# Grouped attention on three engines: a new written-out order, three planner constants, and the heads whose exponential terms are added

## The chip, the cores and the metric

The kernel runs on one core of a Trainium2 chip. A core has TensorE (PE in the profile) for matmuls, ScalarE (ACT) for exponentials, VectorE (DVE) and GpSimd (POOL) for elementwise work, and SyncE (SP), whose queue issues most transfers. The metric is device time in microseconds (us) of one launch. The kernel before took a median of 354.96 us in 3 runs (354.9 to 355.17).

## The reference

Attention with 8 batches, 8 query heads, 2 key/value heads, 1024 positions and a head size of 64, all in float32:

```python
for g in range(n_kv_heads):
    q_group = q[:, g*4 : g*4+4]               # four query heads share one key head
    scores = scale * np.matmul(q_group, k_group.transpose(0, 1, 3, 2))
    attn = np.exp(scores - np.max(scores, axis=-1, keepdims=True))
    attn = attn / (np.sum(attn, axis=-1, keepdims=True) + 1e-08)
    output[:, g*4 : g*4+4] = np.matmul(attn, v_group)
```

So there are 64 heads (batch x query head), each with 1024 x 1024 exponentials. The kernel leaves out the maximum, which the quotient doesn't need for these sizes.

## The kernel before

**Tiling.** A head is cut into 8 score tiles. A score tile has 128 partitions and 2 x 512 columns: line 754 makes it with two matmuls, one for the even query rows against one block of 128 keys and one for the odd rows against the block four further on. The tile lies in one of three slots of PSUM (`sp0` to `sp2`). The exponential of a tile is made in one of two ways.

- On ScalarE: one activation (line 764) writes the tile `pt` in bfloat16.
- On VectorE: one pass (line 775) turns the scores into 16-bit integers `yt`, whose bits read as bfloat16 are a rough exponential. Three steps refine it: line 782 (`zh`) masks the mantissa into `zt`, line 789 (`two`) masks the exponent into `et`, and line 798 (`mul`) multiplies `yt` by `zt`. The exponential is then the sum of two terms, `et` + `zt`. Two tiles usually share a chain (class `Chain`), so that each step works on 2048 columns.

**Values.** Line 816 multiplies 128 queries of a tile with 128 values, which have 64 columns and a column of ones, so that the 65th column sums the exponentials. Eight such pieces of 128 queries make a head. A `pt` tile costs eight matmuls. A VectorE tile costs sixteen, because both terms are multiplied, except in the last TAIL heads: there a fourth step (line 803, `add`) adds the two terms first, and the tile costs eight (lines 267 and 710). Seven pieces share a PSUM bank. VectorE then takes the reciprocal of their sums (line 881, `rec`) and multiplies (line 890, `norm`), and SyncE's queue stores the head (line 894). The first head and the last go through lines 836 and 856, eight matmuls for each tile and term.

**GpSimd.** It multiplies a part of the columns that line 798 would have to (line 732, `gmul`). The part is cut from the end of a chain's columns, and VectorE's own multiply gets what is left. The method `gpsimd` (line 207) is called where VectorE begins a pass or a reciprocal, since VectorE then reads PSUM for a while. It is told how long that lasts, and sizes the part by `w = int((until - at - M_GFIX) / M_GCOL) // GSTEP * GSTEP`, where `until` is the window's end plus M_GOVER and `at` its start plus M_GLEAD. The part waits for the VectorE instruction before the window. GpSimd's queue also issues the loads that cast queries, keys and values to bfloat16 (line 517); SyncE's queue transposes them (lines 576 and 586).

**What sets the order.** The text ORDER (line 64) holds one letter for each decision. For TensorE, `A` is a score tile for ScalarE, `a` to `d` one for VectorE (of the head at hand or of later ones), `V` up to three or four value matmuls, `E` and `L` the values of the first and last head, `F` a matmul that only keeps TensorE busy, `W` waiting. For VectorE, `p` and `P` are a pass, `r` and `R` a reciprocal, `n` a normalization, a digit the next step of that chain, `x` closes a chain early, `i` waits. With `P` and `R` a normalization follows beside the same part of GpSimd. The class `Plan` reads the letters with its constants (lines 11 to 46, in nanoseconds) and turns them into a list of events with planned times. These times fix the sequence on each engine and the place of each transfer in its queue: a query transpose stands 11 us ahead of its head's first score (line 685). On the chip the engines follow their sequences and wait for each other by semaphores, whatever the planned times. M_REC is the planned cost of a reciprocal; M_GFREE is how far a part may reach into VectorE's next instruction before the plan charges for it (line 313).

Of the kernel before, what the change touches and what calls it, by code (L numbers as in the profile page):

```python
# [29 lines left out]
M_D1 = 1.042  # L30
M_D2 = 0.521
M_D4 = 0.261
M_REC = 90
M_GLEAD = 160
M_GFIX = 190
M_GCOL = 1.88
M_GOVER = 100
M_GLATE = 900
M_GFREE = 125
M_ISSUE = 850  # L40
M_OVER = 5000
NEED = 5150
M_GFREE = 125
M_OVER = 5000
NEED = 5150
M_NORM = 531
# [3 lines left out]
PB = 7  # L50
NPIECE = 8
GRAIN = 3
TAIL = 4
CHN = 2
LONG = 6
GFROM = 2
# [5 lines left out]


ORDER = """
AaApFFFFFWFFAWWWWWWWWWWWWWWWWWWWWaWWWWWWWWWWApEEWWAW0WWWbWWWWApEEWWAWW0WWWaEpAEWWA0WWAFWWWWbFF0FE0AE
pAWWWWWWWAR0AWWWWWWWWWaWWWnWWWWWWpWWWWAVVVVVVARnb0VVVVpAVVVVVA0aWWWWApVVVVVVVVAR0AVb0VVVPVVAVVVVnVVA
b0VVVpAVVVVVA0AWWW0WbVVVRVpVVVVAVVVnVVA0bWWWApVVVVVVVVA0AWW0WbVVVRVPVVVVAVVVnVVA0bWWWApVVVVVVVVA0cWW
0WAVVVRVPVVVVAVVVnVAb0WWWWWApVVVVVVVVA0AWW0WWcVVVRpVVVVVAVVnVVVA0bWWWApVVVVVVVVA1cWWWArVPVVVVVVVAnWc
WWA0VpVVVVVVVA0WWcWWApVVVVVVVVAR0AWWWc0VVVVVPVAVVVVVcnAVpVVVAVVV1WVVAcR0WWWWAVPVVVVVVVAnWWAWc0V1VVVV
VpVVAVVVA0bVRVPVVAVVVVVnAA0WVVVV1VVVVVV0AV0VVVVAbVRVPVAVVVVVVVnVAb0WWAVpVVVVVVVVVA0WWWbWA0VVVVVRVPVV  # L70
VAVVVVbnAVpVVVAVVVVV0VVAc1VVVApVVVVVVVA1WbWWWApVVVVVVVVVVA0r1bWWAPVVVVVVVVVAncW0WWAVVVV0VVARVPVVVVVV
AWWnWWWWbA1VVVVVpVVAVVVA1bVRVPVVVAVVVVnVAA00VVVVVAW0WbVVVpVVVVVVAVVrV0cAVpVVVVVAVV0VVAb0VVVVAPVVVVVV
VAncWWW0WAVVVVpVVVVAVVV0VAb0VVVRVpAVVVVVAnbWWW0WAVVVpVVVVAVVVRV1Ab1VVVVAPVVVVVVAnWbWWA0ipVVVVVVVVAR1
cVV1VAVPVVVVAVVVnVVA0bWWWApVVVVVVVVAR1cWWWAPVVVVVVVVVAnbWW0WAVVpVVVVVVVAVV0VVAAR1VVVVVnVVVVVV1cAVpVV
VVVVVA0WWWbWAVpVVVVVVVARWW1WbWWAVPVVVVVVVAnWWcWWA0VVV0VVVVVApVVVVVARW1WbWWAVPVVVVVVVAnWWcWWA0VVVpVVV
VVAVVRV1bAVPVVAVVVVnVAA0VVVV0VVVV0cWAVpVVVVVVVVARW1WbWWAVPVVVVVVVVVAnWcWWA0VVVVpVVVVVVAVV0VcARVPVVVA
VVVnVVA1bVVVpVAVVVVVA01cWWWApVVVVVVVVA0cVARPVVVVVVAnWAV0VVVVV1cWApVVVVVVVVA0cWWWA1VVVVRVPVVVAVVVVnVA
c0WWWApVVVVVVVVAR1cWWWAPVVVVVVVVAnAV1VVVVVVVc2AVpVVVVVVVVVArW0Wc1WWAVVVPVVVVVVAVVnVVVA2cVVpAVVVVVAR0
bVVPVAVVVVVVnAV2AAV1VVVV0VVVVVVA1bVRVPVVVVVAVVnVVVA0cVVVpAVVVVVAR1bWWWAPVVVVVVVVAncWWWA1VVVpVVVAVVVV
0VA1cVRVPVVAVVVVVVnVAa1WWWAVpVVVVVVVVVA0WWWcA1VVVVVpVVVVAVVVVV0VVAbWWWARpVVVVVVVAnAV1VVVVVV0VVVVA0cV  # L80
VVRVPAVVVVVVAnaWW0WWAVVVpVVVVVVAVV0VVA0bVVVVRPVVAVVVVAnWAV0VVVVVVV0bWAVpVVVVVVVARW0WbWAVPVVVVVVVAnWW
bWA0VVVVVpVVVVAVVVV0VVARb0WWWAVPVVVVVVVVVAnWWAWb0VVVVVpVVVAVVVVV0VVARb0WWWWAVPVVVVVVVAnWWbWWA0VVVVpV
VVAVVVV0VVA0bWWWARVPVVVVVVVAnWWbWWA0VVVVpVVVVAVVV0VVA0bWWWARVpVVVVVVVAnWbWWA0VVVVpVVAVVVVV0VVARb0WWW
AVPVVVVVVVAnWWaWWA0VVVVVpVVVVAVVVV0Aa0VVVVVpAVVVVVVAR0WbVVAPVVVVVVVAnAV1VVVVVV0VVAR0aVVVPVVAVVVAnbVi
VipVVVAVVVV0Ab0VVVVVApVVVVVVA0WbWWApVVVVVVVVVVAR1bWWWAPVVVVVVVVVAncWW0WAVpVVVVVVVA0WAVVRV1VVVVVVnVAb
1VVVVpAVVVVVA0bWWWARPVVVVVVVVAnbWWW1WAVVV1VVVVApVVVVVVA0WWbWWARpVVVVVVVVAnaWW1WAVVVpVVVVVAVV0VA0bVVV
RAPVVVVVVAnaV1AVVpVVVVAVVV0VVVAR0bWWWAPVVVVVVVVAnAV1VVVVVVV1VaAipVVVVVVVVVVA0WbWWARPVVVVVVVVVVAnAV1V
VVVVV1bWApVVVVVVVVVARW0WbWWWAPVVVVVVVVAnWbVV1VAVpVVVVVVAV0VVVVA0bWWRWAPVVVVVVVVAnAV1VVVVV1VVbAipVVVV
VVAWWRWW0WcAPVVVVVVVVAnWAWWWb1VVVVpVVVVAVVV0VVAR0cWWWAPVVVVVVVVAnWAWWWb1VVVV1VVVVApVVVVVAW0WWWcWARpV
VVVVVVVAnWcWWWA1VVVVpVVVVAVVV0VVA0cWWWARPVVVVVVVVAnbWWWA1VVVV1VVVVApVVVVVARWW0WbWAPVVVVVVVVAncWWWA1V  # L90
VVpVVVVVAVV0VVVAR0bWWWAPVVVVVVVVAnAV1VVVVVc1WAVpVVVVVVVA0WWbWARPVVVVVVVVAnWAV1VVVVVVb0WAVVpVVVVVVVVA
WW0WWWWcAVRPVVVVVVVAVnVVVb1AVVVpVVAVVVVA1cV0VVpAVVVVVVA1aWWWWARPVVVVVVVVAnbWWW1WAVVVpVVVVAVVVrV2AAnV
VVVV0VV1VVVVA0bVVVVVApVVVVVVVARWnWbWAVpVVVVVVVVVA0WAWWWA0VVVVVV0VVVVVVVrVnVbA0VVVVVVVVVApVVVVVAVV0VV
VAaVVVpVVAVVVVVV0AbWWWArPVVVVVVVVA0AVVnVVVVV0VVVVAAV0VVVVVVVVVVVARnaVVVpVAVVVVVVVVRA0AVnVVVVVV0VVVVV
VA0AVVVVVVVRVV0VVVVVVVVAanWWAVpVxVVVVVVVVVVAR0AWnWAVVV0VVVV0VVVVVL0LLLRnLLLLFFRFn
"""


# [29 lines left out]
class Plan:  # L128
# [78 lines left out]
    def gpsimd(self, s, t, window):  # L207
# [11 lines left out]
        at = max(t, s.tG)  # L219
        until = t + window + M_GOVER  # L220
        at += M_GLEAD
# [19 lines left out]
    def dve(self, s):  # L241
# [14 lines left out]
        if what in "rR":  # L256
            _, _, lo, hi = s.norms[0]
            if s.dq and s.dq[0][0] <= t + M_REC:
                self.gpsimd(s, t, M_REC + 1134 + (M_NORM if what == "R" else 0))
                s.host = True  # L260
            s.ev.append((t, "rec", (lo, hi), None, None))
            end = t + M_REC
            s.dlast = lo
            s.norms[0] = (end, "norm", lo, hi)
        elif what in "pP":
            _, sl, j, c = s.dq.pop(0)
            n = len(STEPS) if j >= nj - TAIL else 3
            if s.open and s.open.nsteps != n:
# [33 lines left out]
        else:  # L302
# [7 lines left out]
            if cols:  # L310
                s.ev.append((t, kind, None, ch.id, n, cols))
                end = at + M_FIX + cols * rate
                end += max(0, s.tB - at - M_GFREE)
            if kind == "zh":
# [26 lines left out]
    def pe(self, s):  # L341
# [4 lines left out]
        if kind in "Aabcd":  # L346
# [12 lines left out]
            else:  # L359
                s.dcount[j] += 1  # L360
                if j == 0:
                    s.twice.append(c)
                if j < nj - TAIL:
                    s.mms[j] += 1
# [73 lines left out]
def kernel(  # L438
# [265 lines left out]
    def terms(j, par, only=range(NC)):  # L704

        for ci in only:
            c = ci if par == 0 else (ci + NH) % NC
            if (j, c) in where:
                ch, i = where[(j, c)]
                if j < NJ - TAIL:  # L710
                    yield ci, et[ch].bitcast(BF16)[:, i, par, :]
# [217 lines left out]
```

## Time and profile before

| | |
|---|---|
| median of 3 runs | 354.96 us |
| profiled execution, its own time | 354.69 us |
| its span, first to last instruction | 352.9 us |
| first exponential on ScalarE begins | 6.22 us |
| last exponential ends | 348.12 us |
| VectorE's last normalization ends | 349.83 us |
| median time of a store to its landing | 3.1 us |
| TensorE clock granted | 1.00 |

The page gives busy time for each engine, a chain of work followed back from the last instruction (each step goes to what released it), and groups of instructions by line and tile. A row such as `L775 DVE TENSOR_SCALAR yt<-sp 128x1024 ... x143 | 172.6, 1207 | 0.6` says: line 775, VectorE, `yt` from `sp`, shape, 143 instructions, 172.6 us busy in all, 1207 ns for one, and 0.6 us of idle time before them. Records of one engine overlap here, one instruction draining while the next begins, so what an instruction costs is the distance from its start to the next start, which is shorter than its record.

### The profile page before, as it was taken

The page shows a single profiled execution, that of the slowest core. Times are in us where ns is not written, and L with a number is a line of the kernel's source. Part 1 is how long each engine was busy: PE and PEld are TensorE (multiplying, and loading weights), DVE is VectorE, ACT ScalarE, POOL GpSimd, SP SyncE. Part 2 cuts the span into 40 slices and gives each one's busy share as a digit, 9 for nine tenths or more (in the row PEclk, how much of TensorE's full clock was granted, in tenths as well). Part 3 has the DMA queues.
Part 4 walks back from the last instruction along what each step waited for, and adds up shares of the span by engine and source line. Part 5 has one row for each costly group of instructions (what it writes and reads, how often), then busy time and mean ns, then how long its engine had stood idle before and what let it go on. Part 6 is the DMA issues. An engine that isn't in the chain of part 4 may idle for free.

```text
span 352.9 us, 14128 instructions
## 1 busy us (share of the span) xinstructions
PE 344.6 (98%) x6247; PEld 223.8 (63%) x6247; DVE 344.3 (98%) x519; ACT 344.3 (98%) x373; POOL 204.1 (58%) x188
## 2 busy tenths in 40 slices
PE   8899999999999999999999999999999999999995
PEld 4456666666666666666666666666666666666664
DVE  4999999999999999999999999999999999999995
ACT  5999999999999999999999999999999999999994
POOL 3157656676577666676766566666657676663000
PEclk9999999999999999999999999999999999999999
DMA  6799666478866987669639756679567885454133
GB/s 150 133 151 151 135 124 136 91 141 146 133 126 124 140 157 132 120 115 154 154 61 181 138 124 115 135 108 180 109 114 130 165 141 112 101 101 114 27 93 121
DMA packets 96430, 44.84 MB, mean 127 GB/s; under 512 B 61152, under 2 KB 95072, under 8 KB 95584
## 3 DMA queue, kind: packets, MB, share of 16 engines
q1 hardware_dynamic: 94128, 31.48, 43.1%
q0 software_dynamic: 2096, 12.19, 24.0%
q8 instruction: 49, 0.80, 1.1%
q10 hardware_dynamic: 144, 0.26, 0.2%
q14 instruction: 13, 0.11, 0.1%
HBM read 27.13 MB, written 28.97 MB: 159 GB/s over the span
## 4 chain that ended last, share of the span: by engine, by line
DVE 67%; PE 21%; ACT 8%; issue 3%; DVEq 0%
DVE yt L775 35%; PE ops L816 10%; DVE et L789 8%; PE sp L754 8%; ACT pt L764 8%; DVE zt L798 7%; DVE ost L890 7%; DVE zt L782 7%; DVE rec L881 2%; PE ops L619 1%; PE sp L856 1%; PE sp L642 0%; DVE kt L663 0%; PE ops L654 0%; PE ops L642 0%
## 5 line engine op out<-in xcount | busy, mean ns | idle before, releaser
L764 ACT ACTIVATE pt<-sp 128x1024 bf16<-128x1024 f32 x369 | 341.8, 1034 | 0.5 <-PE sp L754 0.4
L732 POOL TENSOR_TENSOR zt<-yt,zt 128x464 bf16<-128x464 bf16 (+5 forms) x131 | 173.4, 1324 | 107.7 <-DVE et L789 35.5
L816 PE MATMUL ops<-va,pt 128*128 128x65 bf16 x2848 | 175.1, 194 | 0.0
L754 PE MATMUL sp<-qt,kt 64*128 64x512 bf16 x1024 | 171.0, 382 | 3.2 <-ACT pt L764 1.5
L775 DVE TENSOR_SCALAR yt<-sp 128x1024 uint16<-128x1024 f32 x143 | 172.6, 1207 | 0.6 <-PE sp L754 0.5
L816 PEld LDWEIGHTS <-pt 128*128 128x128 bf16 x2848 | 127.7, 97 | 31.9 <-issue 31.9
L816 PE MATMUL ops<-va,zt 128*128 128x65 bf16 x1120 | 130.9, 194 | 0.0
L816 PE MATMUL ops<-va,et 128*128 128x65 bf16 x1072 | 121.7, 194 | 0.0
L816 PEld LDWEIGHTS <-zt 128*128 128x128 bf16 x1120 | 89.9, 97 | 12.3 <-issue 12.1
L816 PEld LDWEIGHTS <-et 128*128 128x128 bf16 x1072 | 84.2, 98 | 20.6 <-issue 20.6
L754 PEld LDWEIGHTS <-kt 64*128 64x128 bf16 x1024 | 49.2, 93 | 54.8 <-issue 32.5
L782 DVE TENSOR_SCALAR zt<-yt 128x2048 uint16<-128x2048 uint16 x72 | 50.1, 696 | 0.1
L789 DVE TENSOR_SCALAR et<-yt 128x2048 uint16<-128x2048 uint16 x72 | 49.6, 691 | 0.0
L798 DVE TENSOR_TENSOR zt<-yt,zt 128x832 bf16<-128x832 bf16 (+7 forms) x69 | 45.1, 654 | 0.0
L890 DVE TENSOR_TENSOR ost<-ops,rec 128x448 f32<-128x448 f32 (+2 forms) x73 | 44.3, 607 | 0.2
L517 POOL DMA_DIRECT2D qd<-in_q_dram x33 | 20.2, 613 | 4.2 <-PE sp L754 3.3
L881 DVE RECIPROCAL rec<-ops 128x7 f32<-128x7 f32 (+2 forms) x73 | 14.2, 195 | 0.0
L517 POOL DMA_DIRECT2D kd<-in_k_dram x8 | 5.4, 670 | 5.4 <-PE sp L754 5.4
L619 PE MATMUL ops<-warm 128*128 128x128 bf16 (+1 forms) x23 | 4.5, 339 | 1.2 <-DVE warm L511 1.2
L517 POOL DMA_DIRECT2D vd<-in_v_dram x8 | 5.0, 621 | 0.2 <-issue 0.2
L803 DVE TENSOR_TENSOR zt<-et,zt 128x2048 bf16<-128x2048 bf16 (+1 forms) x4 | 4.4, 1090 | 0.1
L619 PEld LDWEIGHTS <-warm 128*128 128x128 bf16 x23 | 2.0, 114 | 3.7 <-issue 2.5
(38 smaller groups left out, 25.2 us busy)
## 6 DMA issues: line engine op xcount, KB each, us to landing
out_dram<-ost SPq DMA_DIRECT2D x64, 256.0 KB, 3.1
qd<-in_q_dram POOLq DMA_DIRECT2D x29, 256.0 KB, 5.0
kt<-kt SPq DMA_DIRECT2D x30, 64.0 KB, 3.1
va<-vd SPq DMA_DIRECT2D x30, 64.0 KB, 3.7
kd<-in_k_dram POOLq DMA_DIRECT2D x7, 256.0 KB, 5.6
vd<-in_v_dram POOLq DMA_DIRECT2D x7, 256.0 KB, 5.2
qt<-qd SPq DMA_TRANSPOSE x63, 4.5
qd<-in_q_dram POOLq DMA_DIRECT2D x5, 128.0 KB, 3.7
```

Of the source, the lines that this page charges most:

```text
L517: return nc.gpsimd.dma_start(out=t.rearrange("(a x) d -> a (x d)", a=128), in_=src.rearrange("(a x) d -> a (x d)", a=128),)
L619: nc.tensor.matmul(ops[bank][:, lo : lo + cols], lhsT=warm[:, 0:128], rhs=warm[:, 0:cols], start=not beside, stop=True, skip_group_check=b ...
L732: gps = nc.gpsimd.tensor_tensor(out=z, in0=flat(yt[j])[:, lo : lo + w], in1=z, op=ALU.mult)
L754: now = nc.tensor.matmul(sps[x][:, half, :], lhsT=t[lo : lo + D, c // NH, ci % NH * 128 : (ci % NH + 1) * 128], rhs=qt[j][lo : lo + D, 0, ...
L764: exps.append(nc.scalar.activation(out=p, in_=where_s[(j, c)], func=AF.Exp, scale=scale))
L775: vec = nc.vector.tensor_scalar(out=yt[ch][:, i, :, :], in0=where_s[c], scalar1=EXP_A, scalar2=EXP_B, op0=ALU.mult, op1=ALU.add,)
L782: vec = nc.vector.tensor_scalar(out=zt[j][:, 0:c], in0=yt[j][:, 0:c], scalar1=0x7F, scalar2=0x3F00, op0=ALU.bitwise_and, op1=ALU.bitwise_or,)
L789: vec = ins = nc.vector.tensor_scalar(out=et[j][:, 0:c], in0=yt[j][:, 0:c], scalar1=0x7F80, scalar2=None, op0=ALU.bitwise_and,)
L798: vec = nc.vector.tensor_tensor(out=z, in0=flat(yt[j])[:, 0 : cols[0]], in1=z, op=ALU.mult)
L816: nc.tensor.matmul(ops[plan.group_of[x] % 2][:, lo : lo + D + 1], lhsT=p[:, qs * 128 : (qs + 1) * 128], rhs=va[(b * G + h // HPG) % NVA][: ...
L881: vec = nc.vector.reciprocal(out=to, in_=sums)
L890: vec = nc.vector.tensor_tensor(out=to, in0=o, in1=by, op=ALU.mult)
```

## The change

The text ORDER is replaced as a whole. Three constants of the plan change (M_REC 90 to 115, M_GOVER 100 to 60, M_GFREE 125 to 85), and TAIL goes from 4 to 3: the two terms are added in heads 61, 62 and 63 and no longer in head 60. No other code changes. Of the 31 lines of the text, the first three and the last are shown.

```diff
-M_REC = 90
+M_REC = 115
 M_GLEAD = 160
 M_GFIX = 190
 M_GCOL = 1.88
-M_GOVER = 100
+M_GOVER = 60
 M_GLATE = 900
-M_GFREE = 125
+M_GFREE = 85
 M_ISSUE = 850
 M_OVER = 5000
 NEED = 5150
-M_GFREE = 125
+M_GFREE = 85
...
-TAIL = 4
+TAIL = 3
 CHN = 2
...
-AaApFFFFFWFFAWWWWWWWWWWWWWWWWWWWWaWWWWWWWWWWApEEWWAW0WWWbWWWWApEEWWAWW0WWWaEpAEWWA0WWAFWWWWbFF0FE0AE
-pAWWWWWWWAR0AWWWWWWWWWaWWWnWWWWWWpWWWWAVVVVVVARnb0VVVVpAVVVVVA0aWWWWApVVVVVVVVAR0AVb0VVVPVVAVVVVnVVA
-b0VVVpAVVVVVA0AWWW0WbVVVRVpVVVVAVVVnVVA0bWWWApVVVVVVVVA0AWW0WbVVVRVPVVVVAVVVnVVA0bWWWApVVVVVVVVA0cWW
...
-VA0AVVVVVVVRVV0VVVVVVVVAanWWAVpVxVVVVVVVVVVAR0AWnWAVVV0VVVV0VVVVVL0LLLRnLLLLFFRFn
+AaApFFFFWWWWFAWWWWWWWWWWWWWWWWWWWWWWWWWWWWaWWWWWWWWWWApEEWWAW0WWWbWWWWApEEWWAW0WWWaWWWWApEEWWA0WWbFF
+WAFFpFEAWWW0WWWAAE0W0WWWWWWWWWWWWWWWaRAnWWWWRWWWPWAVVVVVVVVnA0bWWWWApVVVVVVVVA0aWVpAVVVVVAR0bVVA0VVV
+pVVVAVVVVnVAb0VVVApVVVAV0VVVVA0bVVRVPVVVVVAVVnbV0AVpVVVVVAVV0VVA0bVVRVPVAVVVVVVAnbW0WWAVVpVVVVVVAV0VV
...
+RVV0VVVVVVVVAnAVVV0VVVVVVVVVVVVVVRAnaWWWApVVVVVVVVVxVA0ArVnVVVVVVV0VA0AVVV0VVVVVLLRnLLLLLWWLFFRFn
```

Counted over both texts: `A` 369 before and 370 after, `a` to `d` 143 and 142, `p` and `P` 143 and 142, `V` 1616 and 1608, `n` 74 and 74, `W` 406 and 436, digits 220 and 219, `F` 14 and 13.

More of the change, by code (lines that the diff above doesn't have):

```diff
@@ L64 @@
 ORDER = """
-AaApFFFFFWFFAWWWWWWWWWWWWWWWWWWWWaWWWWWWWWWWApEEWWAW0WWWbWWWWApEEWWAWW0WWWaEpAEWWA0WWAFWWWWbFF0FE0AE
-pAWWWWWWWAR0AWWWWWWWWWaWWWnWWWWWWpWWWWAVVVVVVARnb0VVVVpAVVVVVA0aWWWWApVVVVVVVVAR0AVb0VVVPVVAVVVVnVVA
-b0VVVpAVVVVVA0AWWW0WbVVVRVpVVVVAVVVnVVA0bWWWApVVVVVVVVA0AWW0WbVVVRVPVVVVAVVVnVVA0bWWWApVVVVVVVVA0cWW
-0WAVVVRVPVVVVAVVVnVAb0WWWWWApVVVVVVVVA0AWW0WWcVVVRpVVVVVAVVnVVVA0bWWWApVVVVVVVVA1cWWWArVPVVVVVVVAnWc
-WWA0VpVVVVVVVA0WWcWWApVVVVVVVVAR0AWWWc0VVVVVPVAVVVVVcnAVpVVVAVVV1WVVAcR0WWWWAVPVVVVVVVAnWWAWc0V1VVVV
@@ L70 @@
[L70 to L94, printed above, removed]
@@ L95 @@
-VA0AVVVVVVVRVV0VVVVVVVVAanWWAVpVxVVVVVVVVVVAR0AWnWAVVV0VVVV0VVVVVL0LLLRnLLLLFFRFn
+AaApFFFFWWWWFAWWWWWWWWWWWWWWWWWWWWWWWWWWWWaWWWWWWWWWWApEEWWAW0WWWbWWWWApEEWWAW0WWWaWWWWApEEWWA0WWbFF
+WAFFpFEAWWW0WWWAAE0W0WWWWWWWWWWWWWWWaRAnWWWWRWWWPWAVVVVVVVVnA0bWWWWApVVVVVVVVA0aWVpAVVVVVAR0bVVA0VVV
+pVVVAVVVVnVAb0VVVApVVVAV0VVVVA0bVVRVPVAVVVVVAnbV0AVpVVVVVAVV0VVA0bVVRVPVAVVVVVAnbW0WWAVVpVVVVVVAV0VV
+VVA0bWWRWAPVVVVVVVVAnbW0WWAVVpVVVVAVVV0VVVVA0cWWWRWAPVVVVVVVVAnbW0WWAVVVpVVVAVVV0VVVVAR0cWWWAPVVVVVV
+VVAnbWW0WWAVVVpVVVVVAVV0VAc0VVVRVPAVVVVAnVA0WbVVVpVVVVAVVV0WVVA0bWWWWARPVVVVVVVVAncWWWA0VVVpVVVAVVVV
@@ new lines @@
+0VVA0bVVArPVVVVVVA0WcWWWAPVVVVVVVVAnAV0VVVV0VVVARb0VVVVPVVVAVVVVcnAVpVVVVVAVV0VVAb0VVVVRVAPVVVVVVAnW
+cWWWA0VVVVpVVVVAVVV1VVAc0VARVPVVVVVVAWnWWWbA0VVVVVpVAVVVVVV0VAc0WWWAVpVVVVVVVA0WbWWARVPVVVVVVVAnWWcW
+WA1VVVV0VVApVVVVVVVARWnWbWWApVVVVVVVVA0WcWWWApVVVVVVVVVA1cWWWARPVVVVVVVVVVAncWW1WAVVV2VVVVApVVVVVVVV
+VA00WcWWAVVRVPVVVVVAVVnVVVA1bWWWWApVVVVVVVVA0cWWRWAPVVVVVVVVAncWW01WWAVVpVVVVVVAWV0VcA1VVVVpVAVVVVAR
+0AVVc1VVVPVVVAVVVVnVAc1WWWWAVpVVVVVVVARWW0WcWWAPVVVVVVVVVAnWAV1VVVVVVVV1VcARVPVVVVVVAVnVVVA0cV1VVVVA
@@ new lines @@
+pVVVVVAW1WWWcWApVVVVVVVVA0cWWWARVPVVVVVVVAnWWcWWA1VVVVpVVVVAVVVVR0VAc1WWWAVPVVVVVVVAnWWcWA0VVVVVpVVV
+AVVVVRV0Ac1WWWAVPVVVVVVVAWnWWWcA0VVVVVpVVVAVVVV2AAV0VVVVVV0VbWWARPVVVVVVVVVVAncWWWA1VVVVpVVVVVAVVVVr
+V2VAc2WWWAVPVVVVVVVAnWWWbWA0VpVVVVVVVARWW2WcWWAVPVVVVVVVAnWWbWWA0VVVVpVVVVAVVV0VVAAWWRWWc0VVVVPVVVVA
+VVVnVAA1VVVVV1VVVVVA0bVVVVRVPVVVVAVVVVAnc1VVVApVVVVVVVVA1WWbWWApVVVVVVVVVVAR0c1WWWAVVPVVVVVVAVVnVVVV
+VA0bVVVpAVVVVVAR1bWWWWAPVVVVVVVVAncWW0WWAVVpVVVVVVAVV0VA1bVRVPVVAVVVVVnAA0VVVVV1VVVVVA0bVVpVAVVVVVVR
@@ new lines @@
+A1AVnVVVV1VbWWAipVVVVVVVVA0cWWWARPVVVVVVVVVAnbWWWA1VVVVpVVVVVAVVVV0cA0VVVVApVVVVVVVAR1AVVVnVVVVb1WWA
+VpVVVVVVVVA0WcWAVpVVVVVVVVAR0AWWWbVV0VVVVAPVVVVVVVAncWWARPVVVVVVVAnWWAV1VVVVVV0cWAVpVVVVVVVA1WAWWcRV
+nVVVVVpVVAVVVA01cVVpVAVVVVVV0AAWWW0WcVVVRVPVVVVAVVVnVVA1cWWWApVVVVVVVVA1AWWWbR0VVVVPVVVVAVVVnVVA1cWW
+WApVVVVVVVVAR0WcWWWAPVVVVVVVVAnAV1VVVVVb0WAVpVVVVVVVARW0WcWWAPVVVVVVVVAnbWWWA1VVV0VVVVVApVVVVVVA0WcW
+ARVPVVVVVVVVAnWAV1VVVVVVb0WWAVpVVVVVVVVVARW0WbWWAPVVVVVVVVVVAnAV1VVVVVVb0WAVpVVVVVVVVVARW0WAWWb0VVVV
@@ new lines @@
+VVPVVAVVVVVVVnVAb1WWAVpVVVVVVVA0WWbWARVPVVVVVVVAnWWAV1VVVVVV0VVVA1bVVVpVVAVVVVA0WbVRVPVVVAVVVVVAnA1W
+VVVVVV1VVcAipVVVVVVVVA0WWbVRAPVVVVVAnVVA1bVV1VVVVApVVVVVVA0WbWWARPVVVVVVVVAnAV1VVVVVb1WAVpVVVVVVVARW
+0WaWWAPVVVVVVVVAnbWWWW1WAVVVpVVVVVAVV0VVVA0aWWARPVVVVVVVVVAnAV1VVVVVVVb1AVpVVVVVVVVVARWW0WbWAPVVVVVV
+VAVnVVVVVV1VAb1WWWWAVpVVVVVVVVVA0WWbWARVPVVVVVVVVAnWWbWWA1VVVVVpVVVVAVVV1bAVpVVVVAVV0VAr1cVVPVVAVVVV
+AnAV1VVVVV0VVbARVpVVVVVVAWnWWWcWA1VVVVVpVVVAVVV0VVA0bWWWApVVVVVVVVAR1AWWWc1VVVVVPVVVAVVVVnVAb0WWWAVp
@@ new lines @@
+VVVVVVVARW1WAWWcV1VVVVVPVVAVVVVVnAc0WWWAVpVVVVVVVARWW1WbWAVPVVVVVVVAnWWcWA0VVVVpVVVAVVVV0cAVRpVVAVVV
+VVnVAb1WWWWApVVVVVVVVA0cWWWRWAPVVVVVVVVAnbWW1WWAVVVpVVVVVAVV0VVVARc0WWWAPVVVVVVVVAnbWW1WAVVVpVVVVVVA
+VV0VVAA0VVVV1VVVVVVVRc0AVPVVVVVVVAVnVVVA0bVVVApVVVVVVVVAR1AVVVnVVVVVV0VVVVA1aVVVpVAVVVVVVA0bWWWWARPV
+VVVVVVVAnbWWW1WAVVV1VVVApVVVVVVVA0WbWWARPVVVVVVVVAnbWWW1WAVVVpVVVVVAVV1VAA0VVV0VVVVVVVVVVARnbVVVVpVA
+VVVVVA0b0VVApVVVVVVVVAR0bWWWWAPVVVVVVVVVAnbW0WWAVVpVVVVVVAV0VVAARnVVVVV0VVVVVVVVA1AVVV1VVVVVV0VAAVVV
```

## The prediction

> **What bounds the kernel now.** I read the page first (span, busy shares, chain), then the chain stage by stage, then the groups by shape, then single stretches of VectorE and GpSimd.
>
> ```profile
> span 352.9 us, 14128 instructions
> ...
> PE 344.6 (98%) x6247; PEld 223.8 (63%) x6247; DVE 344.3 (98%) x519; ACT 344.3 (98%) x373; POOL 204.1 (58%) x188
> ...
> DVE 67%; PE 21%; ACT 8%; issue 3%; DVEq 0%
> ```
>
> Three engines are at 98% of the same span, so no idle gap shows a bottleneck; the chain has to tell it. Asked by stages (60 to 120, 240 to 300 and 300 to 348 us), it says:
>
> ```profile
> by line: DVE yt L775 50.1%; DVE et L789 13.1%; DVE zt L798 11.3%; DVE ost L890 10.6%; DVE zt L782 10.6%; issue 2.6%; DVE rec L881 2.4%; DVEq L789 0.0%
> by line: ACT pt L764 47.6%; DVE yt L775 21.2%; DVE ost L890 5.2%; DVE et L789 4.9%; issue 4.4%; DVE zt L798 4.3%; PE ops L816 4.3%; PE sp L754 4.0%; DVE zt L782 3.2%; DVE rec L881 1.0%; DVEq L789 0.0%
> by line: PE ops L816 49.7%; PE sp L754 35.3%; DVE yt L775 7.4%; PE sp L856 2.4%; DVE zt L798 1.8%; DVE zt L782 1.4%; DVE ost L890 1.1%; issue 0.7%; DVE rec L881 0.2%
> ```
>
> VectorE alone sets the pace up to about 200 us, ScalarE for a while after 262, TensorE in the last 48. How much ScalarE has left is seen in the piece of the chain that it carries by itself, against all its exponentials:
>
> ```profile
> 270.05 20.05 ACT pt L764 x22
> L764 ACT ACTIVATE pt<-sp 128x1024 bf16<-128x1024 f32 x369 | 341.8, 1034 | 0.5 <-PE sp L754 0.4
> ```
>
> Free running it needs 20.05 / 22 = 0.911 us per exponential. Over the run it took (348.12 - 6.22) / 369 = 0.927. Records of 1.03 us overlap, so the "0.5 idle" hides 369 x 0.0155 = 5.7 us of small delays, from scores that came late. VectorE's starts, from 6.5 to its last end at 349.8 us, follow each other with only about 1 us idle.
>
> Next, VectorE with GpSimd beside it (first five lines VectorE; the last one GpSimd):
>
> ```profile
> 97.70 0.19 DVE L881 RECIPROCAL rec<-ops 128x7 f32<-128x7 f32 x1
> 97.82 1.17 DVE L775 TENSOR_SCALAR yt<-sp 128x1024 uint16<-128x1024 f32 x1
> 98.91 0.61 DVE L890 TENSOR_TENSOR ost<-ops,rec 128x448 f32<-128x448 f32 x1
> 99.44 0.74 DVE L789 TENSOR_SCALAR et<-yt 128x2048 uint16<-128x2048 uint16 x1
> 100.11 1.21 DVE L775 TENSOR_SCALAR yt<-sp 128x1024 uint16<-128x1024 f32 x1
> ...
> 97.93 1.71 POOL L732 TENSOR_TENSOR zt<-yt,zt 128x800 bf16<-128x800 bf16 x1 [1.24 <-DVE rec L881]
> ```
>
> The reciprocal holds VectorE 0.12 us from start to start (its group: 0.115), not the 0.090 that M_REC says. The GpSimd part ends at 99.64, 0.20 us after the mask L789 began; that mask takes 0.67 to the next start where an undisturbed one takes 0.60. So a part that runs too far into a mask delays VectorE.
>
> **What the Trainium skill says.** "SBUF — State Buffer", section "Two separate sides": VectorE and GpSimd share a port pair by an exclusive lock, and the loser blocks. The trace agrees in part: up to an overlap of about 0.125 us nothing is lost, beyond it VectorE loses one ns for each ns. "VectorE: DVE Perf Modes", section "The perf-mode tier table", gives 693 and 1224 ns for 2048 columns of tensor_scalar and tensor_tensor in bf16; the rows here have 694 to 700 and 1214 to 1222. "Perfetto Trace Analysis", section "Identifying the Most-Contended Engine", warns that matmul busy time is no measure of TensorE's distance from its limit; here matmul is 98% and weight load 63%, so I price TensorE from starts.
>
> **The change, part by part.** Letters of ORDER count the work: A 369 to 370, a/b/c 143 to 142, n 74 both, V 1616 to 1608. Every score tile goes to ScalarE or VectorE (512 in all).
>
> ```profile
> L782 DVE TENSOR_SCALAR zt<-yt 128x2048 uint16<-128x2048 uint16 x71 | 49.7, 700 | 0.1
> L798 DVE TENSOR_TENSOR zt<-yt,zt 128x832 bf16<-128x832 bf16 x20 | 11.5, 576 | 0.0
> L798 DVE TENSOR_TENSOR zt<-yt,zt 128x2048 bf16<-128x2048 bf16 x8 | 9.7, 1214 | 0.0
> L732 POOL TENSOR_TENSOR zt<-yt,zt 128x464 bf16<-128x464 bf16 x66 | 70.1, 1063 | 53.7 <-DVE et L789 25.6 <-DVE zt L782 12.4 <-DVE zt L798 8.9
> L732 POOL TENSOR_TENSOR zt<-yt,zt 128x752 bf16<-128x752 bf16 x28 | 45.0, 1608 | 24.9 <-DVE zt L782 15.9 <-PE sp L754 4.8 <-DVE et L789 3.4
> L732 POOL TENSOR_TENSOR zt<-yt,zt 128x800 bf16<-128x800 bf16 x28 | 47.5, 1698 | 25.4 <-DVE rec L881 14.9 <-DVE zt L782 3.9 <-DVE et L789 3.8
> ```
>
> VectorE:
> - One score pass fewer, 1.13 us (the median of L775 from start to start): -1.13.
> - 72 chains before and after, but two of a single tile in place of one (70 x 2 + 2 = 142). A mask of 1024 columns shows 426 (L782) and 418 ns (L789) against 700 and 694: -0.27 - 0.28 = -0.55.
> - Adds: three of 2048 and one of 1024 become two and one. Start to start one takes 1.14 (336.07 to 337.21): -1.14.
> - Multiplies: 69 both. Walking both orders through gpsimd() (line 207) gives GpSimd 131 parts with 78,912 columns before and 132 with 76,224 after; of 143 x 1024 and 142 x 1024 that leaves VectorE 67,520 and 69,184. At (1214 - 576) / (2048 - 832) = 0.525 ns: +0.87.
> - 74 reciprocals either way; M_REC alters no instruction, only widths and order.
>
> Sum -1.95.
>
> GpSimd's ends: the width is (window + M_GOVER - 160 - 190) / 1.88, cut to 8. Beside a pass: (1134 + 100 - 350) / 1.88 gives 464, with 60 it gives 448; with a normalization of 531 more, 752 becomes 728; with the reciprocal, 90 becomes 115 and 100 becomes 60: 800 becomes 792. At (1698 - 1063) / 336 = 1.89 ns per column they end 30, 45 and 15 ns sooner. For each part I took its end minus the start of the next mask or multiply on VectorE, in the trace. Above 0.125 lie 8 of 65, 15 of 27 and 21 of 27 (three parts have no such successor); the excess sums to 0.41, 0.93 and 1.46 us (measured loss 0.14, 0.87, 1.45). Shifted, 0.19, 0.30 and 1.17 stay: 2.80 to 1.65, **-1.14**. Unknown: whether the ends of parts move so evenly; between 0 and -2.5.
>
> So VectorE -3.1 in all. ScalarE one exponential more: +0.91 at its free rate, hidden as long as its 5.7 us of delays shrink, +0.93 if they don't. TensorE: 8 matmuls more of L816 (a VectorE tile outside the last heads costs 16, one inside 8: 5184 to 5192) at 30 ns between starts, +0.24; one dummy fewer, -0.1; turns between scores and values 503 to 497 at 0.1 (two score matmuls to the next value matmul 0.32 us, of which 0.23 is theirs), -0.6: -0.5 together. But in the last heads two tiles more carry two terms: 16 matmuls, +0.5 just where TensorE leads.
>
> Loads: after 6 us no engine shows a wait for one. The query transposes are issued 11 us ahead by line 685 and land in 4.5 (a median), so 6 us cover the shifts; without that cover one late head costs up to 4.5. Up to the first V the new order has 15 exponentials and 6 passes as before. Live exponential tiles need 20 of 34 buffers (21 before). I take 0 for both.
>
> Passing it on: shares of the chain as weights, 0.67 x -3.1 + 0.21 x -0.5 + 0.08 x 0.9 = **-2.1**. Against it: adds and half chains (-1.69) lie in the last stage, where VectorE has 12% of the chain; 0.55 x 1.69 comes back, +0.9, and 85% of 0.5 for the 16 matmuls, +0.4. In the old end two groups of eight matmuls (L856, at 348.20 and 348.45) follow the last exponential, in the new one only its own: -0.2. That makes -1.0. The new order may fit its end to this, so I take the middle of -2.1 and -1.0: **-1.5**. On the profiled execution 354.69 gives 353.19; that execution was 0.27 below the median of 354.96, from which I forecast 354.96 - 1.5 = 353.4.
>
> **Rivals.**
> - VectorE's whole saving goes through. For it: it leads for 200 us, and ScalarE has 5.7 us to give. Against: the last 90 us are not its own. 354.96 - 3.1 = 351.9.
> - GpSimd's parts do not end sooner for VectorE: they start when VectorE's counter lets them (the 800 parts 0.26 us after the reciprocal's start, not at the 0.16 of M_GLEAD), and a new order can start them later. Then 0.67 x 1.14 = 0.8 of the gain is missing: 354.96 - 1.5 + 0.8 = 354.3.
> - The end eats it: two-term tiles and the last values keep TensorE to the old end. 354.9, no difference.
> - Slower: the fixed alternation on TensorE, not VectorE's work, sets the pace. For it: TensorE has 85% of the last chain. Then ScalarE keeps 0.927 us and runs 370 times: 355.9. It decides when the mean spacing doesn't fall by 0.927 / 370 = 2.5 ns.
>
> **How the numbers follow.** Forecast 0.55, whole saving 0.13, GpSimd 0.07, end eats it 0.14, slower 0.11. A measurement here can tell about 0.2%, 0.7 us: faster means under 354.25, slower over 355.67. Half of the GpSimd case is under 354.25: faster 0.72, same 0.17, slower 0.11. The range takes in the first three and the unchanged one, 351.8 to 355.3, and leaves out the slower case; the forecast alone covers 352.3 to 354.2.
>
> **What would show it.** Right: VectorE's L775 x142, L803 x3, L798 with 808 and 872 columns as the commonest; masks L782 and L789 with means nearer 690; exponentials spaced 0.920 to 0.922 from 6.2 us to a last end near 346.8. Wrong: a spacing still at 0.927; a wait of TensorE's scores for ScalarE or VectorE much over today's 1.5 us; a wait for a query or value load; GpSimd parts that overlap the masks by 0.2 us as now; more than 4.8 us between the last exponential and the end of the span.

## The result, and the profile after

The changed kernel takes 353.8 us (median of 7 runs, 353.5 to 354.11) against 354.93 for the kernel before (7 runs). The ratio is 0.9969, with a 95% interval of 0.9959 to 0.998. It is faster by 0.3%, 1.1 us of the 1.5 forecast. In a later measurement the same two kernels gave 0.9971 (0.996 to 0.9982); below I use 0.9970, or -1.06 us on 354.8.

The page of the kernel after: span, busy shares, chain.

```profile
span 351.7 us, 14152 instructions
...
PE 343.8 (98%) x6254; PEld 223.4 (64%) x6254; DVE 342.6 (97%) x517; ACT 343.5 (98%) x374; POOL 199.7 (57%) x189
...
PE 44%; ACT 34%; DVE 19%; issue 1%; DMA 1%; DVEq 0%
```

Busy shares tell as little as before, but the chain has turned over: VectorE fell from 67% to 19%, ScalarE rose from 8% to 34%. The chain of the kernel after by stages (6.2 to 60, 60 to 120, 300 to 347 us):

```profile
by line: ACT pt L764 94.0%; PE ops L816 3.3%; PE sp L754 3.0%; issue 0.2%
by line: PE ops L816 53.8%; PE sp L754 46.3%; issue 0.0%
by line: ACT pt L764 47.0%; PE ops L816 31.7%; PE sp L754 19.7%; PE sp L856 2.8%; issue 0.2%
```

From 60 to 120 us, where VectorE led alone before, TensorE leads now, and ScalarE leads ahead of that stage. The groups of the kernel after that answer to those shown of before:

```profile
L764 ACT ACTIVATE pt<-sp 128x1024 bf16<-128x1024 f32 x370 | 340.9, 1038 | 0.5 <-PE sp L754 0.4
L782 DVE TENSOR_SCALAR zt<-yt 128x2048 uint16<-128x2048 uint16 x70 | 49.3, 705 | 0.1
L789 DVE TENSOR_SCALAR et<-yt 128x2048 uint16<-128x2048 uint16 x70 | 47.8, 688 | 0.0
L732 POOL TENSOR_TENSOR zt<-yt,zt 128x792 bf16<-128x792 bf16 x27 | 45.4, 1683 | 24.8 <-DVE rec L881 15.2 <-PE sp L754 4.4 <-DVE zt L782 4.0
```

One exponential more takes 0.9 us less of ScalarE's time (341.8 to 340.9). From the first exponential to the last one's end it is 341.13 us (6.05 to 347.18) after 341.90; the mean spacing, from one start to the next, is 0.9216 us after 0.9263. From the last exponential's end to the end of the span it is 4.54 us after 4.80. Together -1.03 us; the first exponential began at another moment in every profile (5.78 to 6.50 us in those below), which is chance. The mask L782 did not get shorter (700 to 705 ns) and L789 only a little (694 to 688). Run 8 shows what part of the missing gain lies there.

### The profile page after: what moved, and what is told of

The parts are those of the page before. It is cut to its first block, busy times and chain, and to the rows that moved or that the text cites. A ratio compares the mean times of both kernels' runs of the same rounds, so it can differ in the third digit from the quotient of the medians.

```text
span 351.7 us, 14152 instructions
## 1 busy us (share of the span) xinstructions
PE 343.8 (98%) x6254; PEld 223.4 (64%) x6254; DVE 342.6 (97%) x517; ACT 343.5 (98%) x374; POOL 199.7 (57%) x189
## 4 chain that ended last, share of the span: by engine, by line
PE 44%; ACT 34%; DVE 19%; issue 1%; DMA 1%; DVEq 0%
ACT pt L764 34%; PE ops L816 24%; PE sp L754 19%; DVE yt L775 10%; DVE ost L890 2%; DVE zt L782 2%; DVE et L789 2%; DVE zt L798 2%; DMA q<-in_q_dram 1%; PE sp L856 1%; DVE rec L881 1%; PE sp L642 0%; ACT q L631 0%; DVE qt L660 0%; DVE kt L661 0%
## 5 line engine op out<-in xcount | busy, mean ns | idle before, releaser
L764 ACT ACTIVATE pt<-sp 128x1024 bf16<-128x1024 f32 x370 | 340.9, 1038 | 0.5 <-PE sp L754 0.4
L732 POOL TENSOR_TENSOR zt<-yt,zt 128x448 bf16<-128x448 bf16 (+6 forms) x132 | 168.4, 1276 | 110.2 <-DVE et L789 39.5
L816 PE MATMUL ops<-va,zt 128*128 128x65 bf16 x1112 | 128.8, 194 | 0.0
L816 PEld LDWEIGHTS <-zt 128*128 128x128 bf16 x1112 | 88.2, 97 | 11.6 <-issue 11.6
L782 DVE TENSOR_SCALAR zt<-yt 128x2048 uint16<-128x2048 uint16 (+1 forms) x72 | 50.2, 697 | 0.2
L789 DVE TENSOR_SCALAR et<-yt 128x2048 uint16<-128x2048 uint16 (+1 forms) x72 | 48.7, 681 | 0.0
L798 DVE TENSOR_TENSOR zt<-yt,zt 128x872 bf16<-128x872 bf16 (+12 forms) x69 | 45.4, 659 | 0.0
L517 POOL DMA_DIRECT2D qd<-in_q_dram x33 | 21.3, 646 | 3.7 <-PE sp L754 2.9
L803 DVE TENSOR_TENSOR zt<-et,zt 128x2048 bf16<-128x2048 bf16 (+1 forms) x3 | 3.1, 1043 | 0.0
```

Source lines behind the costliest of these rows:

```text
L517: return nc.gpsimd.dma_start(out=t.rearrange("(a x) d -> a (x d)", a=128), in_=src.rearrange("(a x) d -> a (x d)", a=128),)
L732: gps = nc.gpsimd.tensor_tensor(out=z, in0=flat(yt[j])[:, lo : lo + w], in1=z, op=ALU.mult)
L764: exps.append(nc.scalar.activation(out=p, in_=where_s[(j, c)], func=AF.Exp, scale=scale))
L782: vec = nc.vector.tensor_scalar(out=zt[j][:, 0:c], in0=yt[j][:, 0:c], scalar1=0x7F, scalar2=0x3F00, op0=ALU.bitwise_and, op1=ALU.bitwise_or,)
L789: vec = ins = nc.vector.tensor_scalar(out=et[j][:, 0:c], in0=yt[j][:, 0:c], scalar1=0x7F80, scalar2=None, op0=ALU.bitwise_and,)
L798: vec = nc.vector.tensor_tensor(out=z, in0=flat(yt[j])[:, 0 : cols[0]], in1=z, op=ALU.mult)
```

## Experiments

Twelve runs. Each is compared with the kernel before by its ratio; a difference to the changed kernel is that of the two ratios, times 354.8 us.

**1 and 2: VectorE lighter, in both kernels.** The edit, the same in both:

```diff
-            z = flat(zt[j])[:, 0 : cols[0]]
+            m = max(16, cols[0] - 128)
+            z = flat(zt[j])[:, 0:m]
             vec = nc.vector.tensor_tensor(
-                out=z, in0=flat(yt[j])[:, 0 : cols[0]], in1=z, op=ALU.mult
+                out=z, in0=flat(yt[j])[:, 0:m], in1=z, op=ALU.mult
```

> The kernel before, with 128 columns fewer in nearly every multiply of VectorE (line 798): 8,816 columns x 0.525 ns = 4.6 us less work for VectorE, the order and everything else as it is. It leaves that part of the products out. If the chain's shares are prices (VectorE 67% before), the time falls by about 3.1 us. If the order on TensorE sets the pace whatever VectorE costs, it doesn't move. If all three engines share the end about equally, it falls by some 1.5 us.

> The changed kernel with the same cut: 8,768 columns, 4.6 us less work for VectorE, that part of the products left out. If VectorE went off the path with the change (19% of the chain), the time falls by about 0.9 us against the changed kernel; if VectorE still sets the pace, by about 3 us as in the kernel before; if the order sets the pace, by nothing.

The kernel before went to 0.9947 (0.9929 to 0.9964), -1.9 us; the changed one to 0.9953 (0.9938 to 0.9967), only 0.6 us under itself. Chain and exponentials, first of the lighter kernel before, then of the lighter changed one:

```profile
ACT 87%; PE 10%; DMA 1%; issue 1%; DVE 0%
...
L764 ACT ACTIVATE pt<-sp 128x1024 bf16<-128x1024 f32 x369 | 340.1, 1036 | 0.6 <-PE sp L754 0.6
```

```profile
ACT 89%; PE 9%; issue 1%; DVE 0%
...
L764 ACT ACTIVATE pt<-sp 128x1024 bf16<-128x1024 f32 x370 | 340.6, 1038 | 0.3 <-PE sp L754 0.3
```

VectorE is gone from both chains and ScalarE carries nearly 90%. Yet the exponentials don't come down to the 0.911 us that the forecast took as free running. They stop at a mean spacing of 0.9212 and 0.9202. So about 2.0 us were to be had before the change (0.9263 - 0.9207 over 369), not 5.7, and the changed kernel (0.9216) stands 0.5 us above this floor.

The floor is not ScalarE's own rate, though the chain books it on ScalarE. In the lighter changed kernel 67 of the 369 spacings are longer than 0.924 us, 0.961 on average. The other 302 average 0.911, and those of the two kernels without the cut 0.911 and 0.912. Here is one late exponential of the lighter changed kernel, with the exponential ahead of it and TensorE's work in between (single rows of the view by time):

```profile
257.18 1.03 ACT L764 ACTIVATE pt<-sp 128x1024 bf16<-128x1024 f32 x1
257.58 0.19 PE L817 MATMUL ops<-va,pt 128*128 128x65 bf16 x1
257.71 0.39 PE L754 MATMUL sp<-qt,kt 64*128 64x512 bf16 x2
258.14 1.02 ACT L764 ACTIVATE pt<-sp 128x1024 bf16<-128x1024 f32 x1
```

The score matmuls end at 258.10 and the exponential starts 0.04 us later, 0.96 us after the one ahead of it. It waited for its scores, which stood behind value matmuls in TensorE's sequence. Of the 67 late ones 59 start within 0.03 us of the signal from their scores, and in 54 of these TensorE came straight from value matmuls, with no wait of its own just before. Such a delay shows neither as idle time nor in the chain: the record of the exponential ahead lasts until 258.21, so the chain goes on along ScalarE. Before the change 90 spacings were late and cost 5.4 us over 0.911; in the lighter kernel before, 74 are left and cost 3.7 us. VectorE's cut took away 1.7 us of these delays and left the rest.

**3 and 4: TensorE lighter, in both.**

```diff
             for i in range(j, j + c):
                 ci, p = every[i]
+                nmm[0] += 1
+                if nmm[0] % 34 == 0 and 0 < i < len(every) - 1:
+                    continue
```

> The kernel before without 115 of its 5,040 value matmuls of line 816, spread evenly: 115 x 0.031 us = 3.6 us less for TensorE. It leaves those products out. By the chain's shares (TensorE 21%) the time falls by 0.75 us; if the order on TensorE sets the pace, by up to 3.6 us.

> The changed kernel without 122 of its 5,048 value matmuls of line 816, spread evenly: 3.8 us less for TensorE, those products left out. By the chain's shares (TensorE 44%) the time falls by 1.7 us against the changed kernel, more than in the kernel before; if TensorE sets the pace alone, by 3.8 us; if ScalarE does by now, by nothing.

Before: 0.9996 (0.9988 to 1.0005), no change. Changed: 0.996 (0.9945 to 0.9974), 0.36 us under the changed kernel, within the uncertainty; its exponentials come to a spacing of 0.9203. TensorE's 21% and 44% of the chains are not prices: 3.6 us of its work taken away evenly are worth 0.1 to 0.4 us.

**5 and 6: ScalarE heavier, in both.**

```diff
+            if len(exps) % 16 == 0:
+                nc.scalar.activation(out=extra, in_=warm[:, 0:8], func=AF.Copy)
```

> The kernel before with a small extra activation (8 columns, into a buffer that nothing reads) on ScalarE behind every sixteenth exponential: 23 of them, by the small activations of the start (0.38 us for 256 columns, 0.42 for another) some 0.2 us each, so 4 to 5 us more for ScalarE. If ScalarE has 5.7 us to give before the change, as forecast, at most 0.5 us of it shows. If its own limit is the 0.920 us per exponential that the lighter VectorE left (2.3 us to give), 2 to 3 us show.

> The changed kernel with the same 23 extra activations, 4 to 5 us more for ScalarE. If ScalarE became the limit with the change (0.9216 us per exponential against 0.920), nearly all of it shows, 3.5 to 5 us against the changed kernel; if it has 3.9 us to give down to 0.911, about 1 us.

Before: 1.0013 (1.0007 to 1.002), +0.5 us. Changed: 1.0005 (0.9997 to 1.0014), +1.2 us against the changed kernel. The sizes are lower than expected because the work was: the group and the chain of the heavier changed kernel.

```profile
ACT 92%; PE 6%; issue 1%; DVE 0%
...
L767 ACT ACTIVATE extra<-warm 128x8 bf16<-128x8 bf16 x23 | 5.0, 217 | 0.0
```

A record of 0.217 us adds only 0.09 us to the spacing of the exponentials around it (1.010 from one to the next, for 0.920), so 2.1 us in all. About a fifth of that showed before the change, more than half after it. ScalarE's work became dearer with the change.

**7: the changed kernel once more, as reference.**

> The changed kernel as it is, on the same chip as its variants: 353.8 us, 1.1 us under the kernel before.

353.64 us (median of 8 runs), ratio 0.9971. Its profiled execution was the slowest of them, 354.98. Its first exponential came 0.38 us later than in the other profile of this kernel; the rest has one reason, VectorE at 89 us:

```profile
89.16 0.69 DVE L789 TENSOR_SCALAR et<-yt 128x2048 uint16<-128x2048 uint16 x1 [0.95 <-DMA out_dram<-ost]
```

A mask that keeps old stores in check (line 795) waited 0.95 us for a store. Counted from the first one, every later exponential is about 1.05 us late against the other profile, up to the end. At 0.911 in place of 0.9216 ScalarE would make that up in about 100 exponentials (an estimate), and some 270 follow: one more sign that the pace is not ScalarE's alone.

**8: GpSimd's parts sized by when they start.** In the changed kernel I looked at VectorE and GpSimd beside a reciprocal (first four lines VectorE, then the GpSimd part, then a row of that line's own view):

```profile
134.20 0.20 DVE L881 RECIPROCAL rec<-ops 128x7 f32<-128x7 f32 x1
134.32 1.21 DVE L775 TENSOR_SCALAR yt<-sp 128x1024 uint16<-128x1024 f32 x1
135.44 0.61 DVE L890 TENSOR_TENSOR ost<-ops,rec 128x448 f32<-128x448 f32 x1
135.98 0.72 DVE L789 TENSOR_SCALAR et<-yt 128x2048 uint16<-128x2048 uint16 x1
...
134.47 1.68 POOL L732 TENSOR_TENSOR zt<-yt,zt 128x792 bf16<-128x792 bf16 x1 [1.21 <-DVE rec L881]
...
L732 POOLq EVENT_SEMAPHORE  x58: 17/43/43, 52.3 to 319.7; - x58
```

By the code the part waits for the VectorE instruction ahead of the reciprocal; the view names the reciprocal. It begins 0.27 us after the reciprocal's start, where M_GLEAD plans 0.16, and ends at 136.15, 0.17 us into the mask. Of the 132 parts, those with an extra waiting instruction (the last line) in front begin 0.17 us after the VectorE instruction that they wait for ended; the others 0.08. The extra ones belong to first parts of a chain, almost without exception: these wait for TensorE's and GpSimd's own earlier use of the buffers too. Among the 792 wide parts 25 of 27 are first ones; among the 800 wide ones before the change 22 of 28 were. So their overlap hardly fell (median 206 to 192 ns). Counted as in the prediction (what is over 0.125 us, summed over all parts), VectorE lost 2.8 us to overlaps before the change and 2.2 after it, not 1.65. The edit sizes by that:

```diff
     plan = Plan(NJ, NPT - 2, NCT - 1, NYT - 2)
+    respread(plan, lambda w, first: w + ({448: -16, 728: -16, 792: -48} if first
+                                         else {448: 32, 728: 24, 792: 8}).get(w, 0))
```

Here `respread` goes over the plan's list, gives each part its new width and VectorE's multiply what is left; the order is untouched.

> The changed kernel with GpSimd's parts sized by when they start: the first part of a chain, which starts 0.09 us late, 48 columns less beside a reciprocal and 16 less elsewhere; later parts 32, 24 or 8 more. VectorE's columns stay about the same, and of the 1.7 us that the overlaps cost it some 1.4 us go. By VectorE's price in the changed kernel (0.76 us for 4.6 us of work) about 0.25 us less than the changed kernel, hardly to be told from none; if the overlaps delay the end themselves, 1 us less.

352.86 us (4 runs, 352.83 to 353.39), ratio 0.9953 (0.9938 to 0.9968): 0.6 us under the changed kernel. The two intervals overlap a little, but three of the four runs (352.83 to 352.88) lie below all 15 runs of the changed kernel, whose fastest took 353.18. The loss to overlaps fell from 2.2 to 0.4 us with VectorE's multiplied columns the same (69,184 and 69,192). The chain, and the same stretch in this kernel, whose lines stand some 25 further down:

```profile
ACT 89%; PE 8%; DMA 1%; issue 1%; DVE 0%
...
134.31 0.20 DVE L906 RECIPROCAL rec<-ops 128x7 f32<-128x7 f32 x1
136.12 0.68 DVE L814 TENSOR_SCALAR et<-yt 128x2048 uint16<-128x2048 uint16 x1
...
134.58 1.58 POOL L757 TENSOR_TENSOR zt<-yt,zt 128x744 bf16<-128x744 bf16 x1 [1.20 <-DVE rec L906]
```

The mask is back at 0.68, the part ends 0.04 us into it, and the spacing is 0.9201, at the floor of run 2. Expected was 0.25 us, from VectorE's price in run 2. That price was too low, because 4.6 us were more than the floor lets through: the 1.8 us of this run already yield as much.

**9 to 12: parts of the change by themselves.** The shorter GpSimd parts in the old order (the same `respread`, with 448 for 464, 728 for 752, 792 for 800):

> The kernel before in its own order, with GpSimd's parts cut as in the change (464 to 448, 752 to 728, 800 to 792) and VectorE's multiplies taking the columns: 66 x 16 + 28 x 24 + 28 x 8 = 1,952 columns, +1.0 us of work against some 1.1 us of overlap saved. Nothing within 0.3 us, if work and overlap weigh alike; 0.5 us faster or more if an overlap costs the end more than the same time spread evenly.

Ratio 0.9997 (0.9989 to 1.0004), no change, and a chain as before:

```profile
DVE 76%; PE 18%; issue 4%; DMA 1%; SPq 0%; DVEq 0%
```

Losses fell by 1.2 us and the multiplies took 1,880 columns, 1.0 us. The reverse in the changed kernel, with the widths of before:

> The changed kernel with GpSimd's parts as long as before (448 to 464, 728 to 752, 792 to 800) and VectorE's multiplies shorter by 1,920 columns (-1.0 us): overlaps cost VectorE about 1.0 us more. About 0.3 us slower than the changed kernel, 0.8 us under the kernel before, if overlaps weigh more than even work; no change if alike. If the shorter parts made the change's gain, the kernel before's 354.7 us comes back.

Ratio 0.9978 (0.9971 to 0.9985), still 0.8 us faster than before; the 0.28 us to the changed kernel are within the uncertainty. Losses are 3.3 us in place of 2.2, with 1,808 columns fewer to multiply.

**Run 11**, the old order with its parts sized by when they start (first parts of 464, 752 and 800 columns 32, 40 and 48 less, later ones of 464 16 more):

> The kernel before in its own order, with GpSimd's parts sized by when they start: a chain's first part 32, 40 or 48 columns less (464, 752, 800), later parts of 464 columns 16 more. VectorE's columns grow by about 1,400 (+0.75 us), its loss to overlaps falls from 2.7 to some 0.3 us: 1.6 us less. If the time now hangs on VectorE, some 0.9 to 1.5 us faster than before, so that the old order comes within 0.5 us of the changed kernel; if the gain of the change came from the order, no faster than 0.4 us.

Ratio 0.9969 (0.9957 to 0.9981), as good as the whole change without a new order. The losses fell from 2.8 to 0.2 us; with 1,592 columns more (+0.8 us) VectorE's steps take 1.4 us less. The chain is ScalarE's:

```profile
ACT 77%; PE 20%; DMA 1%; issue 1%; DVE 0%
```

And TAIL by itself: the old order without the add of head 60.

```diff
+    at = next(e for e in plan.ev if e[1] == "add")
+    plan.ev.remove(at)
...
-                if j < NJ - TAIL:
+                if j < NJ - TAIL + 1:
```

(Each piece of head 60 then runs over ten terms in place of eight.)

> The kernel before without the add of head 60: its two tiles give two terms, 16 more value matmuls in the last 20 us (+0.5 us for TensorE), and VectorE has one add of 1.14 us less. If the end hangs on TensorE, as forecast, 0.3 to 0.5 us slower; if on VectorE, up to 0.8 us faster; if on ScalarE's last exponentials, no change.

Ratio 1.0008 (1.0002 to 1.0015), +0.28 us (0.1 to 0.5). An add of 1.14 us less did not make up for the 16 matmuls more.

## Why the prediction was right, and where not

The direction, the range and the time hold: 353.8 for 353.4. By its steps:

- **VectorE's own work**: the counts hold (142 passes, three adds, 69,184 columns to multiply), and line 803 takes 4.02 us from start to start in all before, 2.88 after, -1.14. The stretch from VectorE's first pass to its last normalization got shorter by only 0.95 us. The prediction's 1.95 us and the measured 0.6 us of overlaps make a saving of some 2.5 us (an estimate); the rest of it became waits.
- **Overlaps with GpSimd, -1.14**: mis-sized, measured -0.6. The step moved every part's end by the columns cut. The first parts of chains start 0.09 us later than the others, and the new order puts more of them beside reciprocals. One of the prediction's signs of being wrong came true: parts beside reciprocals still overlap the masks by 0.19 us. The rival that named the late start had the mechanism; run 8, which removes most of these overlaps, shows what they held back: 0.6 us.
- **ScalarE has 5.7 us to give**: the sum was right, the step from it was not. The spacings that are not late average 0.909 to 0.912 us in every kernel, and most of the delays are waits for late scores, as the prediction said. But it took all of them for something that VectorE's saving can shrink. With 4.6 us less on VectorE 3.7 us of delay remain before the change, and nearly all the late scores stand right behind value matmuls in TensorE's sequence. So about 2.0 us were to be had, of which the exponential more takes 0.92. With the 0.26 us of the end, 1.3 us were open to this change by this sum, 1.7 by run 8. The rival of the whole saving, 351.9, was out of reach.
- **Passing it on by shares of the chain**: the rule failed as a rule, though 0.67 for VectorE came out near. Down to the floor VectorE's work goes through for the most part (1.4 us less in run 11, the old order with its parts sized by when they start: 1.1 faster), beyond it hardly at all. TensorE's share promised 0.75 us of 3.6 and gave 0.1. ScalarE's promised 0.08 and took a fifth.
- **TensorE's count**: 5184 and 5192 include the first and the last head; line 816 itself has 5040 and 5048. The 8 more are right.
- **The end**: 0.2 forecast for the last exponential, 0.26 found; 0.4 for two-term tiles, 0.28 found when tried alone.
- **The slower rival**, that the order alone sets the pace: excluded by run 1, and by a spacing that fell by 4.7 ns. What remains at the floor is of its kind, though: scores that TensorE's sequence brings late.

That the size came near is in part luck. -2.1 came from weights that are no prices, the corrections for the end from the same weights, and -1.5 is the middle of -2.1 and -1.0, taken without a measurement to say how far the new order mends its end.

Two things stay open. One is what would lower the floor: three different reliefs of the changed kernel (VectorE lighter, TensorE lighter, the overlaps gone) end at a spacing of 0.9201 to 0.9203, and no run lightens two engines at once. The other is what the gain is made of. Neither the shorter parts alone (no change) nor TAIL alone (+0.28) makes it, and the new order with the long parts keeps 0.8 of 1.06 us. By elimination it lies in the new order with one tile fewer on VectorE. How much of that the planned cost of the reciprocal brought to the search can't be told, since it acts through the order; it was not tried by itself.

## What to carry to other kernels

When several engines are busy all the time, the chain's shares name the one that leads but don't price the others; cut a few us of work out of one engine, see where the next floor stands, and forecast no gain beyond it. An engine's delays are not all there for the taking: find out what each waits for before counting on it. Compare the start of an instruction with the end of its input, because where records overlap, short waits appear neither as idle time nor in the chain. Where two engines hand a shared resource back and forth by planned times, compare planned and traced starts by kind of wait: one constant for all of them hid 0.09 us in nearly half the cases, and sizing by it gave as much as a new order.

## What was not expected of the hardware

A GpSimd multiply with a separate waiting instruction in front starts 0.17 us after the VectorE instruction it waits for, in place of 0.08 (medians of 58 and 74 in the kernel after). VectorE's masks and multiplies lose nothing to a GpSimd instruction that ends up to 0.125 us after their start, and about one ns for each ns beyond: masks of 2048 columns take 0.60 us to the next start below that, 0.63 at overlaps of 0.150 to 0.175 and 0.66 at 0.175 to 0.200. A small activation between exponentials has a record of 0.217 us and costs 0.09. The first exponential begins anywhere from 5.78 to 6.50 us in the profiles; whether that makes the scatter between the other runs isn't shown.
